# Sliding-window copy: half a batch more through on-chip memory, one opening load, other splits of the direct copies

## The chip, the cores and the metric

The kernel runs on one core of a Trainium2 chip. The metric is device time in microseconds; "before" is quoted as the median of its runs. They were taken in four groups, and the same kernel takes 745 to 755 us from one group to another, so every kernel is compared only with runs of its own group. I call the group of the prediction group 0 (before: 751.7 us) and the three groups of experiments 1, 2 and 3.

## The reference

```
batch, length, dim = 32, 4096, 256        # float32; window_size 64, stride 32
n_windows = (length - window_size) // stride + 1        # 127
for i in range(n_windows):
    result[:, i] = x[:, i * 32 : i * 32 + 64]
```

Each batch is 128 blocks of 32 rows (32 KB each). A window is two neighbouring blocks, so nearly every block is written twice: 134 MB come in, 266 MB go out, nothing is computed.

## The kernel before

Two kinds of copying run side by side. **Direct** batches (21 of 32) go from HBM to HBM, issued on the SP queue, 16 windows at a time, in packets of 32 KB. **Staged** batches (11) are loaded once into on-chip memory (SBUF) and stored twice, on the ACT queue, in packets of 16 KB. The leftovers of the direct batches, 15 windows each ("remainders"), are issued last, on the POOL queue.

```
def load(self, q, g):                          # staged: one tile of 128 blocks
    ...
    parts = [(k, 4, 32, 1) for k in range(4)] if g == 0 else [(0, step, n, step)]
    for rows in parts:                         # (first partition, step, count, unit)
        self.issue(self.c.load(q, self.tiles[i], b, c, rows), self.loaded[i])
...
staged = [*range(1, B, 3)]
...
for i, (b, w) in enumerate(sixteens):          # direct: groups of 16 windows
    loading = turns < first_loads or 0 <= second < loads
    share += 120 if turns < 16 or -8 <= second < 16 else 90 if loading else 18
    if share >= 120:                           # split: two DMAs of 16 packets of 32 KB
        share -= 120
        turns += 4
        count(c.windows(ring_d, b, w, 16, 0), done)
        count(c.windows(ring_d, b, w, 16, 1), sem)
    else:                                      # whole: one DMA of 32 packets of 32 KB
        turns += 3
        count(c.windows(ring_d, b, w, 16), sem)
...
ring_r.wait_ge(near, 16)                       # remainders, when the direct groups are nearly done
for b, w, n in edges:
    ...
    count(c.windows(ring_r, b, w, n), rest)
```

`turns` counts packets, in sixteens. The semaphore write at the end of a DMA is a packet too: on the SP and ACT queues the trace has 3264 and 656 packets of 4 bytes for 204 and 41 DMAs, 16 for each. So a split group is 4 sixteens of packets for its 1024 KB and a whole one 3. The two queues passed packets about one for one: from 120 to 400 us 3294 (SP) and 3292 (ACT), semaphore writes included (2078 and 3100 without them), though one moved 67.61 MB and the other 50.79 (lines below). At that pace packets per byte set each queue's part of the bytes: a split group moves fewer direct bytes per turn than a whole one, and the staged queue gets more of the time. A hand count that alternates packets, with durations from the trace (1.235 and 0.62 us), puts the last packet at 743.5 us, and the trace has it at 745.8 us.

## Time and profile before

| | before, group 0 |
|---|---|
| time, median | 751.7 us |
| DMA bytes | 313.26 MB |
| HBM read and written | 488.0 MB |
| first and last data packet | 2.4 and 745.8 us |

From the page of before, the lines on the DMA engines in 40 slices (DMA is the busy share in tenths), the packets, the queues (q1 is SP, q10 is ACT, q0 is POOL) and HBM:

```profile
DMA  8999999999999999999999999999999999999996
...
DMA packets 18290, 313.26 MB, mean 418 GB/s; under 512 B 4336, under 2 KB 4336, under 8 KB 4528
...
HBM read 220.95 MB, written 267.09 MB: 651 GB/s over the span
```

The engines are busy between the first slice and the last (busy share 1.00 to 1.02 in the stretches below), so time is bytes over rate. The same by stretch (us from the start; then length, POOL busy, clock, DMA busy share, GB/s). A packet is counted whole where it starts, so a short stretch can show a few per cent too much, as a busy share of 1.02 tells. The stretches from 32 and 425 us are those of staged loads, those from 120 and 540 us of staged stores, that from 660 us of the remainders:

```profile
14.00:32.00 18.00, 0.00 (x0) 1.00 1.02 400
32.00:120.00 88.00, 0.00 (x0) 1.00 1.01 428
120.00:400.00 280.00, 0.00 (x0) 1.00 1.01 423
425.00:520.00 95.00, 0.00 (x0) 1.00 1.00 429
540.00:650.00 110.00, 0.00 (x0) 1.00 1.01 422
660.00:735.00 75.00, 6.95 (x13) 1.00 1.01 420
```

The rate is lower where direct copies have a larger part: 428 and 429 GB/s in the load stretches, 423 and 422 in the store stretches. The DMA view of before for 120 to 400 us (queue, packets, MB, share of the engines) shows direct at 67.61 of 118.40 MB, 57%; in the load stretches it is 53%:

```profile
q1 hardware_dynamic: 3294, 67.61, 57.4%
q10 hardware_dynamic: 3292, 50.79, 43.2%
```

**How I add up a trace.** A packet's time has a shortest common value for its size: 1.213 us for 32 KB, 0.611 for 16 KB, 0.159 for 4 KB, 0.084 for 2 KB, 0.009 for a semaphore write. The sum of these over all packets, divided by 16 engines, I call the *floor*; what packets take above it, also over 16, the *excess*. Idle engine time at the start and at the end (fewer than 16 packets under way) comes on top; overlap (more than 16 under way) comes off. For before: floor 729.6 + excess 15.0 + idle 5.3 - overlap 4.1 = 745.8 us, the last packet. The floor depends on bytes and packet sizes alone. Each sum is of one traced run. The five or six runs of one kernel in its group spread over 0.5 us (before_again) to 4.9 us (no_half), so a difference of 1 us in excess between two single traces shows little unless others repeat it. The span ends 3.6 us after that packet; of these the SP queue waits 1.7 us for POOL's and 0.6 us for PE's.

### The profile page before, as it was taken

How to read it: one execution, taken by the hardware profiler on the slowest of the kernel's cores; microseconds unless marked ns; L12 is line 12 of the kernel's file. 1: busy time of each engine (PE TensorE's matmuls, PEld its weight loads, DVE VectorE, ACT ScalarE, POOL GpSimd, SP SyncE). 2: the span in 40 equal slices, each digit the busy share in tenths (PEclk: the TensorE clock that was granted, in tenths of full speed). 3: DMA queues.
4: the chain of work that ended last, by engine and by line, in shares of the span. 5: the costliest groups of instructions: out<-in, count | busy, mean ns of one | idle time of the engine just before them, and what ended most of it. 6: DMA issues, size and time to landing. Idle time of an engine off the chain costs nothing.

```text
span 749.4 us, 322 instructions
## 1 busy us (share of the span) xinstructions
POOL 12.8 (2%) x26
## 2 busy tenths in 40 slices
POOL 0000000000000000000000000000000000040100
DMA  8999999999999999999999999999999999999996
GB/s 360 401 427 429 427 429 428 434 423 418 420 424 423 418 424 415 422 427 427 414 427 417 429 432 429 430 422 430 429 423 421 423 421 419 425 426 423 431 409 262
DMA packets 18290, 313.26 MB, mean 418 GB/s; under 512 B 4336, under 2 KB 4336, under 8 KB 4528
## 3 DMA queue, kind: packets, MB, share of 16 engines
q1 hardware_dynamic: 8016, 154.32, 48.8%
q10 hardware_dynamic: 9104, 138.41, 44.0%
q0 software_dynamic: 1168, 20.51, 6.5%
q14 instruction: 2, 0.02, 0.0%
HBM read 220.95 MB, written 267.09 MB: 651 GB/s over the span
## 4 chain that ended last, share of the span: by engine, by line
another core or an unknown queue 92%; POOL 2%; issue 0%; POOLq 0%; SPq 0%
POOL out_dram L34 2%; POOL out_dram L44 0%; POOLq L236 0%; SPq L172 0%; POOLq L114 0%
## 5 line engine op out<-in xcount | busy, mean ns | idle before, releaser
L34 POOL DMA_DIRECT2D out_dram<-in_x_dram x21 | 12.0, 576 | 691.3 <-DMA out_dram<-in_x_dram 654.0
L44 POOL DMA_DIRECT2D out_dram<-in_x_dram x1 | 0.6, 581 | 0.0
L222 POOL MEMSET const-float32-0.0<- 128x1 f32 x1 | 0.1, 98 | 0.2 <-issue 0.2
L222 POOL MEMSET const-bfloat16-1.0<- 128x1 bf16 x1 | 0.1, 101 | 0.0
L222 POOL MEMSET const-float32-1.0<- 128x1 f32 x1 | 0.1, 98 | 0.0
L222 POOL MEMSET const-uint8-127<- 128x1 uint8 x1 | 0.1, 98 | 0.0
## 6 DMA issues: line engine op xcount, KB each, us to landing
out_dram<-in_x_dram SPq DMA_DIRECT2D x92, 1024.0 KB, 100.7
out_dram<-xb ACTq DMA_DIRECT2D x21, 4096.0 KB, 139.7
out_dram<-in_x_dram SPq DMA_DIRECT2D x110, 512.0 KB, 90.3
xb<-in_x_dram ACTq DMA_DIRECT2D x10, 4096.0 KB, 131.4
out_dram<-in_x_dram POOLq DMA_DIRECT2D x20, 960.0 KB, 38.5
xb<-in_x_dram ACTq DMA_DIRECT2D x4, 1024.0 KB, 15.7
out_dram<-xb ACTq DMA_DIRECT2D x2, 1024.0 KB, 113.4
out_dram<-xb ACTq DMA_DIRECT2D x4, 512.0 KB, 96.9
```

The costliest lines, as they stand in the source:

```text
L34: return q.dma_start(out=self.oap((b * self.nw + w0) * 2 + h, [[2 * blk, n], row]), in_=self.xap(b * self.nb + w0 + h, [[blk, n], row]), m ...
L44: return q.dma_start(out=self.oap((b * self.nw + w0) * 2, [[part, 16], [2 * self.blk, n], row]), in_=self.xap(b * self.nb + w0, [[part, 16 ...
L222: nc = _bacc.Bacc("TRN2", target_bir_lowering=False, num_devices=1)
```

## The change

Its intent: stage half of batch 0 as well, so that fewer bytes pass HBM twice; slow the direct side (more split groups, 73 of 143 instead of 55 of 147, and every third remainder in 16 KB pieces), so that both sides still end together; and load the first tile in one DMA instead of four.

```
-        parts = [(k, 4, 32, 1) for k in range(4)] if g == 0 else [(0, step, n, step)]
-        for rows in parts:
-            self.issue(self.c.load(q, self.tiles[i], b, c, rows), self.loaded[i])
+        self.issue(self.c.load(q, self.tiles[i], b, c, (0, step, n, step)), self.loaded[i])
...
+    items.insert(6, (0, 1, c.nb // 2))
...
-        w = 15 if b - 1 in staged else 0
+        w = c.nb // 2 + 1 if b == 0 else 15 if b - 1 in staged else 0
...            # singles, edges, loads, last columns follow from the half batch
-            share += 120 if turns < 16 or -8 <= second < 16 else 90 if loading else 18
+            share += 120 if turns < 16 or -8 <= second < 16 else 104 if loading else 35
...
-            count(c.windows(ring_r, b, w, n), rest)
+            count(c.windows(ring_r, b, w, n, None, 16384 if i % 3 == 2 else DIRECT), rest)
```

More of the change, by code (lines that the diff above doesn't have):

```diff
@@ L162 @@
     for b in direct:
-        w = 15 if b - 1 in staged else 0
+        w = c.nb // 2 + 1 if b == 0 else 15 if b - 1 in staged else 0
         sixteens += [(b, w + 16 * j) for j in range((c.nw - w) // 16)]
-    singles = [(B - 1, c.nw - 1, 1)]
-    edges = [(b, 0 if b - 1 in staged else 112, 15) for b in direct[:-1]]
+    singles = [(0, 0, 0), (0, c.nb // 2, 1), (B - 1, c.nw - 1, 1)]
+    edges = [(b, 0 if b - 1 in staged else 112, 15) for b in direct[1:-1]] + [(0, 113, 14)]
     last = B - 2
-    edges.append((last, 112, 4))
-    first_loads, loads, stores = 6 * 17, 5 * 17, 6 * 34
+    edges.append((last, 112, 5))
+    first_loads, loads, stores = 6 * 17, 5 * 17 + 9, 6 * 34
     turns = share = 0
@@ L192 @@
         ring_r.wait_ge(near, 16)
-        for b, w, n in edges:
+        for i, (b, w, n) in enumerate(edges):
             for k in (b - 1, b + 1):
@@ L196 @@
                     st.wait_stored(ring_r, place[k])
-            count(c.windows(ring_r, b, w, n), rest)
-        count(c.columns(ring_r, last, 116, 9), rest)
+            count(c.windows(ring_r, b, w, n, None, 16384 if i % 3 == 2 else DIRECT), rest)
+        count(c.columns(ring_r, last, 117, 8), rest)
         st.wait_stored(ring_d, place[B - 1])
```

## The prediction

> **What bounds it now.** Nothing computes; the 16 DMA engines do. The page's DMA row is 9 in 38 of 40 slices; by stretch (busy share and rate per window) DMA is 100% busy from 14 us to 735 us and all packets have ended at 746 us[...]. So time = bytes / rate plus about 2.4 us before the first packet and 3 to 4 us of tail. 313.26 MB move, 418 GB/s mean. HBM itself sees 488 MB (651 GB/s), as a direct byte is read and written there, while a staged byte touches HBM once per transfer.
>
> The rate is not one number. In the two load stretches (32 to 120, 425 to 520 us) it is 428 to 429 GB/s, with the direct queue moving 53% of the bytes; in the store stretches (120 to 400, 540 to 650) 422 to 423 with 57%; during the remainders (660 to 735) 420 with 58%. Single packets say the same: a 32 KB direct one takes 1.216 to 1.218 us in the loads, 1.240 to 1.245 in the stores, 1.249 with the remainders; staged 16 KB ones 0.616 to 0.628; the shortest common values are 1.213 and 0.611. Between 655 and 659 us, staged alone, every packet takes 0.611. So the more direct traffic in the mix, the slower each packet, by 2 to 3%. That waiting is what the change can win. [...]
>
> **What it adds and removes.**
> - Half a batch more is loaded first: 64 x 32 KB = 2.10 MB more DMA bytes (315.36 MB). At 420 GB/s: +5.0 us, all critical, since the engines are never idle. A count of alternating packets with the trace's durations (1.235 and 0.62 us) gives 743.5 us for before's last packet (746 in the trace) and 748.7 for after: +5.1 us.
> - HBM bytes fall by 2.10 MB; the direct share of all bytes falls from 55.8% to 54.1%.
> - More direct groups split in two halves (73 of 143, was 55 of 147): the direct queue moves fewer bytes per turn. Store stretches fall by about 1.6 points of share, loads by 0.8.
> - A third of the remainders in 16 KB pieces: the mean share there falls by about 4 points.
>
> Gain: the two kinds of stretch give 1.4 GB/s per point, perhaps 2 on the steep side. Stores: 2.3 to 3.2 GB/s over 405 us is 2.2 to 3.1 us; remainders 1.3 us (4 to 7 GB/s over 85 us); loads 0.3 us. Together about 4 to 4.7 us.
> - Opening load in one DMA: saves about 2 us of issue on the ACT queue[...]. From 16 to 30 us staged packets take 0.72 to 0.85 us; if that belongs to the first whole-tile load it moves earlier. Worth within 1 us.
>
> Balance: the count has the staged queue end 5 us after the remainders; as it still feeds all engines this costs little.
>
> **Predicted:** 751.0 us, 80% between 747 and 755. Faster by over 2%: 0.01; same: 0.98; slower: 0.01.
>
> **What would show it.** 315.36 MB; store stretches at 425 to 426 GB/s and 32 KB packets near 1.230; remainders at 424 or more; loads unchanged; last packet near 745 us; tail no longer.
>
> **What would make it wrong.** If packets in store stretches stay at 1.24 us, the full 5 us shows (756). If they fall to 1.22, 747. A tail in which one queue alone, or few engines, remain; a worse opening.

## The result, and the profile after

752.87 us against 751.74 us, medians of six runs each. The ratio is 1.0009, interval 0.9987 to 1.0031: the same. (A ratio is the mean time of one kernel's runs over that of the other's of the same rounds, so not quite the ratio of the medians.) The page of after:

```profile
DMA  9999999999999999999999999999999999999996
...
DMA packets 19042, 315.36 MB, mean 420 GB/s; under 512 B 4626, under 2 KB 4626, under 8 KB 4834
...
HBM read 218.86 MB, written 267.09 MB: 647 GB/s over the span
```

Its stretches, and the queues for 120 to 400 us:

```profile
14.00:32.00 18.00, 0.00 (x0) 1.00 1.03 435
32.00:120.00 88.00, 0.00 (x0) 1.00 1.00 426
120.00:400.00 280.00, 0.00 (x0) 1.00 1.01 423
425.00:520.00 95.00, 0.00 (x0) 1.00 1.01 427
540.00:650.00 110.00, 0.00 (x0) 1.00 1.01 425
660.00:735.00 75.00, 3.96 (x7) 1.00 1.00 421
```

```profile
q1 hardware_dynamic: 3426, 65.67, 56.0%
q10 hardware_dynamic: 3423, 52.68, 44.6%
```

More bytes at a slightly better mean rate. The large step is not where I looked for it: it is the opening (400 to 435 GB/s), while the long store stretch did not move. The sums, in us per engine:

| trace | floor | excess (to 35 us / 35 to 650 / later) | idle start + end | last packet |
|---|---|---|---|---|
| before, group 0 | 729.6 | 15.0 (2.2 / 10.5 / 2.3) | 2.6 + 2.6 | 745.8 |
| after, group 0 | 734.8 | 12.2 (0.8 / 9.8 / 1.6) | 2.3 + 2.5 | 747.7 |

So 5.2 us of bytes were added and 2.8 us of waiting taken away: half from the opening, a quarter each from the long middle and from the remainders. In the two store stretches alone, the excess fell from 8.4 to 7.9 us.

### The profile page after: what moved, and what is told of

Its sections match the earlier page's. It is cut to its first block, busy times and chain, and to the rows that moved or that the text cites. A ratio compares the mean times of both kernels' runs of the same rounds, so it can differ in the third digit from the quotient of the medians.

```text
span 751.2 us, 338 instructions
## 1 busy us (share of the span) xinstructions
POOL 12.8 (2%) x26
## 4 chain that ended last, share of the span: by engine, by line
another core or an unknown queue 92%; POOL 2%; issue 0%; POOLq 0%; SPq 0%
POOL out_dram L34 2%; POOL out_dram L44 0%; POOLq L235 0%; SPq L171 0%; POOLq L112 0%
```

## The experiments

My theory: the half batch costs its 5.2 us everywhere, and the other three parts each take away some waiting and keep the ends together. Rivals: a part does nothing, the gain is chance, or the half batch alone does the work.

### Group 1: one part alone or undone (before 754.88 us)

**open_one**: before, with the opening load in one DMA.

```
-        parts = [(k, 4, 32, 1) for k in range(4)] if g == 0 else [(0, step, n, step)]
-        ...
+        self.issue(self.c.load(q, self.tiles[i], b, c, (0, step, n, step)), self.loaded[i])
```

> The kernel before with only the opening load changed to one DMA. Theory (the four strided opening loads make the first whole-tile load slow: packets of 0.72 to 0.85 us between 16 and 30 us, which the changed kernel lacks): 14 to 32 us runs near 430 GB/s instead of 400, the sum of packet time above the shortest durations falls by about 1.4 us per engine in the first 35 us, and the time is 750.2 to 750.6 us against 751.7. Rival (the opening's gain is by chance or is given back later): 751.7 us, within 0.3.

754.74 us, ratio 1.0002 (0.9987 to 1.0017). The opening is fast, as expected (stretch view of this run), and excess to 35 us is 1.0 us:

```profile
14.00:32.00 18.00, 0.00 (x0) 1.00 1.01 429
```

The total did not follow. In this trace the direct queue gets its first packet at 5.7 us, not at 2.4 us as in before. In the two traces of group 0 the order differs the same way: with one load the staged packets start at 2.0 us and the direct ones at 5.7 us, with four loads the direct ones start at 2.4 us and the staged ones at 4.0 us. The remainders start at 664.5 us (658.7 in before of group 0), and excess after 650 us is 3.6 us, the highest of this group, with direct copies in the majority at the end. That the opening's gain was given back there is the likely reading. It was not isolated, as group 1 has no trace of before.

**four_back**: the changed kernel, with the opening in four loads again.

> The changed kernel with the opening load in four strided DMAs again. Theory: 1.4 us slower than the changed kernel, 754.1 us, with 14 to 32 us near 400 GB/s. Rival (the fast opening of the changed kernel comes from the other split of the direct side, not from the load): as the changed kernel, 752.7 us.

754.23 us, ratio to before 0.9996 (0.9982 to 1.0010). The changed kernel itself was not in this group, so the expected difference in time was not tested. The trace was read: 412 GB/s from 14 to 32 us, excess to 35 us 1.7 us, against 0.8 to 1.0 us in the three kernels of this group with one load. The slow opening follows the four loads, not the other parts of the change. This kernel serves below as the reference of group 1 for the middle and the end.

```profile
14.00:32.00 18.00, 0.00 (x0) 1.00 1.02 412
660.00:735.00 75.00, 3.96 (x7) 1.00 1.01 429
```

**pieces_off**: the changed kernel with all remainders in 32 KB pieces.

```
-            count(c.windows(ring_r, b, w, n, None, 16384 if i % 3 == 2 else DIRECT), rest)
+            count(c.windows(ring_r, b, w, n, None, DIRECT), rest)
```

> The changed kernel with all remainders in 32 KB pieces. Theory (smaller pieces lower the direct share, hence packets wait less): 660 to 735 us falls towards the 420 GB/s of before, excess packet time after 650 us rises by about 0.7 us per engine: 753.4 us. Rival (the pieces serve the balance of the ends alone): the remainders end some 7 us before the staged queue by my count (737 and 749 us at unchanged packet times), the staged queue ends alone with packets of 0.611 us, and the time is 752.7 us or less.

757.82 us, ratio 1.0041 (1.0024 to 1.0057). The stretch view has the remainders back at the old rate:

```profile
660.00:735.00 75.00, 4.13 (x8) 1.00 1.00 419
```

Excess after 650 us is 2.9 us, against 1.1 us in four_back: the pieces do take waiting away, more than the 0.7 us expected. And the rival was right about the order of the ends, but wrong about its price: the staged queue ends last and alone (752.0 us, the remainders at 748.2), with at most one packet at a time in its last 3 us, and idle time at the end is 5.5 us against 2.7.

**shares_back**: the changed kernel with the old shares of split groups.

```
-            share += ... 104 if loading else 35
+            share += ... 90 if loading else 18
```

> The changed kernel with the old shares of split groups (90 and 18 of 120). Theory (the lower direct share of the mix speeds up the store stretches): excess packet time in the store stretches rises by 0.5 to 1.5 us per engine, the direct side ends about 10 to 15 us before the staged side, partly made up by staged packets alone at 0.611 us: 753 to 754 us. Rival (the slow packets come in bursts that the mix doesn't govern): 752.7 us, within 0.3.

758.64 us, ratio 1.0060 (1.0038 to 1.0081). Excess from 35 to 650 us is 12.7 us, against 10.2 in four_back and 9.9 in pieces_off, the same bytes on the same chip: splitting more groups takes some 2.5 us of waiting away. Of these, 1.0 to 1.4 us are in the two store stretches, as the theory had it. The rest of the expectation missed: the kernel is 3.8 us slower than before, not 1.3 to 2.3, and the direct side ends 2 to 4 us before the staged side, not 10 to 15. Here too the staged queue ends alone, and the idle time at the end is 4.6 us.

### Group 2: the half batch alone, the opening, a rebalanced mix (before 745.16 us)

**after_again**: the changed kernel, unchanged.

> The changed kernel once more, on the same chip as the others of this group, as the chips of the two earlier groups differ (before took 751.7 us on one and 754.9 us on the other). Theory (the changed kernel's sum is 5.2 us more bytes against about 3 us less waiting, wherever it runs): 0.5 to 2 us slower than before. Rival (waiting differs from chip to chip; where before waits more, the lower direct share wins more): same as before or up to 2 us faster where before takes 754 us or more. The slow spell at 330 to 400 us of its first trace (excess 2.4 us per engine) comes back at the same place if it is of the kernel, and does not if it is chance.

747.87 us, ratio 1.0037 (1.0025 to 1.0049): slower by 0.4%, with an interval clear of 1. The 2.7 us by the medians are more than the 0.5 to 2 us expected; the rival spoke of a before at 754 us or more, which this group does not have. In this group packets wait far less: excess 5.0 us in all, against 12.2 in group 0. The spell at 330 to 400 us has 0.8 us, not the 2.4 us of group 0, so at that size it is not of the kernel.

**half_alone**: of the change, only the half batch (four loads, old shares, no small pieces).

> The changed kernel with the opening in four loads, the old shares and no small pieces, so the half batch alone. Theory (the other parts of the change only put the ends back together and lower the waiting): shortest-duration sum 5.2 us above before, the direct side through about 19 us before the staged side by count at unchanged packet times (730 against 749), excess as before or 1 us less, tail idle 4 to 6 us instead of 2.6: 7 to 10 us slower than before. Rival (the half batch by itself lowers the waiting as it takes the direct traffic off): 3 to 5 us slower.

751.45 us, ratio 1.0080 (1.0063 to 1.0097): 6.3 us slower by the medians, a little less than the theory's range and more than the rival's. The direct groups are through earlier, the remainders start at 638.9 us (650.3 in after_again), the staged queue ends last at 747.2 us (the remainders at 744.6, not 19 us earlier), and idle time at the end is 5.9 us against 4.3. Excess is 8.3 us against 5.0 in after_again: the half batch alone does not bring the low waiting of the whole change. Before has no trace in this group; in group 3, at nearly the same time, its excess is 7.7 us.

**open_rows**: before, each of the four opening loads on 32 consecutive partitions.

```
-        parts = [(k, 4, 32, 1) for k in range(4)] if g == 0 else ...
+        parts = [(32 * k, 1, 32, 1) for k in range(4)] if g == 0 else ...
```

> The kernel before with its opening still in four loads, but each of 32 consecutive partitions instead of every fourth. Theory A (the stride is to blame for slow staged packets at 16 to 30 us): 14 to 32 us near 430 GB/s. Theory B (four small loads ahead of the whole ones, with the direct queue getting its first packets at 2.4 us instead of 5.7, set the engines' phase so that the first whole load is slow): 14 to 32 us at 400 to 412 GB/s again. Time within 1 us of before in both cases.

750.93 us, ratio 1.0076 (1.0057 to 1.0095). Both theories fell, and the time is outside what either allowed:

```profile
2.00:14.00 12.00, 0.00 (x0) 1.00 1.01 276
14.00:29.00 15.00, 0.00 (x0) 1.00 1.03 336
32.00:120.00 88.00, 0.00 (x0) 1.00 1.00 431
```

(This trace is of the slowest of six runs, 2.5 us above the median.) Staged packets take 1.02 us on average until 29 us, and 0.613 us from there to 40 us. The last of the four loads lands at 30.9 us. This made me look again at before: its four loads land at 9.6, 15.2, 20.6 and 27.7 us, the one load of the changed kernel at 20.8 us. So the slow packets of 16 to 27.7 us in before are the third and fourth opening load themselves. They are not "the first whole-tile load", as the prediction and my first expectation had it; only those from 28 to 32 us (0.71 us) are of that load. The timeline shows the same from the other side: the first store waits for that tile, and the ACT queue issues it at 27.75 us in before,

```profile
27.75 22.24 ACTq L63 DMA_DIRECT2D out_dram<-xb  x1
```

and at 20.81 us in after:

```profile
20.81 15.46 ACTq L63 DMA_DIRECT2D out_dram<-xb  x1
```

Most of these 7 us are not slow packets, though. In group 3 the staged packets of before take 0.63 us from 16 to 28 us, hardly more than the shortest, and its first store is still issued at 26.07 us, against 20.86 in after_same. There, too, the direct queue gets its first packet earlier with four loads (2.4 us, with one load 5.6).

In this trace the loads of 32 consecutive partitions are slow from the start: 276 GB/s from 2 to 14 us, where the loads of every fourth partition have 396 in before of group 0 and 395 in group 3. By my count of its packets it moves 208 to 213 GB/s from 2 to 6 us, with no direct packets running yet. Why is not shown. Nor is it shown why the loads of every fourth partition are slow in group 0, from the third on (400 GB/s from 14 to 32 us, 435 with one load), and hardly in group 3 (422 and 437); the trace does not tell which engine a packet ran on.

**open_bal**: open_one with fewer split groups (72 and 12 of 120), so that the late direct side catches up.

> The kernel before with one opening load, and fewer split groups (72 and 12 of 120), so that the direct side, which starts 3.3 us later with the one load, is through earlier. Theory (the opening's gain of 1.2 us was given back because the direct side ended alone, with excess of 2.8 us after 700 us against 1.4): both sides end together again, excess after 700 us near 1.5, and the time is 1 to 2 us below before. Rival (the higher direct share takes the gain back in the store stretches): within 0.5 us of before.

744.78 us, ratio 0.9991 (0.9977 to 1.0004). The two sides end together (739.5 and 739.2 us), excess after 700 us is 0.8 us, but the time is within noise of before. Of the two theories the rival holds: about 0.4 us by the medians is no win that five rounds can show. Its reason holds too, on single traces: excess from 35 to 650 us is 6.3 us, against 5.4 in open_rows, which has before's shares.

### Group 3: both kernels traced on one chip, no half batch, no staging (before 745.30 us)

**before_again** and **after_same**: the two kernels, unchanged.

> The kernel before once more, to have its trace on the same chip as the changed kernel's[...]. Sum of shortest packet times 729.8 us per engine on any chip; excess between 8 us (a quiet chip) and 19 us; time 745 to 755 us. Theory: excess here is the number that sets what the change costs.

> The changed kernel on the same chip as the kernel before. Theory (5.2 us more bytes against waiting that shrinks in proportion, by 20 to 35%, with one opening load, lower direct share and smaller remainders): excess 3 to 5 us less than before where before has 15 to 18 us (time 0 to 2 us above before), 2.5 to 3 us less where before has 8 to 9 us (time 2 to 3 us above before). Rival (the gain is a fixed amount that doesn't depend on the chip): excess 2.8 us less, time 1 to 1.5 us above, whatever before's excess.

745.57 us (ratio 1.0005) and 748.03 us (1.0038, interval 1.0026 to 1.0050). Their sums:

| trace | floor | excess (to 35 us / 35 to 650 / later) | idle start + end | last packet |
|---|---|---|---|---|
| before, group 3 | 729.6 | 7.7 (1.0 / 5.0 / 1.7) | 2.7 + 4.3 | 740.2 |
| after, group 3 | 734.8 | 5.5 (0.8 / 3.4 / 1.3) | 2.2 + 4.0 | 742.2 |

The same +5.2 us of floor, and 2.2 us less excess. The time came out where the theory put it (2 to 3 us above), but the loss of excess is smaller than either expectation: 2.2 of 7.7 us here and 2.8 of 15.0 in group 0 are neither a fixed amount nor a fixed part. The stretches of the store side, before:

```profile
120.00:400.00 280.00, 0.00 (x0) 1.00 1.00 427
540.00:650.00 110.00, 0.42 (x1) 1.00 1.00 427
660.00:735.00 75.00, 2.30 (x4) 1.00 1.00 420
```

and after:

```profile
120.00:400.00 280.00, 0.00 (x0) 1.00 1.01 428
540.00:650.00 110.00, 3.84 (x7) 1.00 1.00 428
660.00:735.00 75.00, 3.70 (x7) 1.00 1.01 424
```

Why packets wait half as long here as in group 0 (another chip or another neighbour, say), nothing I ran shows.

**no_half**: one opening load, the new shares, the small pieces, but eleven staged batches.

> Everything of the change but the half batch: one opening load, shares 104 and 35, small pieces, with eleven staged batches. Theory (the half batch is there to keep the two sides ending together once the direct side is slowed): the staged side ends some 12 to 14 us before the direct side (730 and 744 us by count at unchanged packet times), the direct side alone has long packets (1.3 us or more per 32 KB), excess falls by 2 us or more up to 700 us but comes back after it; time within 1.5 us of before. Rival (the half batch is dead weight): no_half keeps the lower excess and is 2 to 5 us faster than before.

750.88 us, ratio 1.0074 (1.0057 to 1.0091). The rival falls, and of the theory only the order of the ends holds. It is 5.6 us slower than before, not within 1.5. The excess up to 700 us did not fall by 2 us or more: it is 6.5 us, in before_again 6.2 (from 35 to 650 us it is 4.7 against 5.0). Nearly all staged packets are through by about 716 us and the remainders run on alone until 748.7 us, 30 us after the staged side and not 12 to 14. (This trace is of the slowest of six runs, 3.1 us above the median, so its tail is longer than the usual one.)

```profile
660.00:705.00 45.00, 12.70 (x22) 1.00 1.01 422
705.00:716.00 11.00, 0.00 (x0) 1.00 1.05 390
716.00:740.00 24.00, 0.00 (x0) 1.00 0.96 318
```

In that last stretch 32 KB packets take 1.56 us on average and the rate is 318 GB/s; excess after 650 us is 7.6 us against 1.7, and idle time at the end 7.7 us against 4.3. Once the direct side has been slowed, the half batch pays for itself by taking work off it: with it (after_same) the time is 2.9 us shorter.

**direct_only**: before without staging, every window copied from HBM to HBM, no group split.

> No staging at all: every window copied straight, 266 MB of packets instead of 313 MB, 32 batches. If packets kept 1.213 us per 32 KB it would take about 625 us. Theory (packets wait because HBM serves every direct byte twice): with direct traffic alone the HBM rate stays near the 650 to 680 GB/s of the mix, packets take 1.5 to 1.65 us, time 780 to 830 us. Rival (waiting comes from bursts that have nothing to do with the HBM rate): packets near 1.25 us, about 650 us.

809.56 us (one run, one look), as the theory expected; the rival's 650 us falls. The engines move only 266 MB, floor 618.7 us, but excess is 177 us:

```profile
100.00:700.00 600.00, 0.00 (x0) 1.00 1.00 334
```

```profile
HBM read 266.34 MB, written 266.34 MB: 659 GB/s over the span
```

334 GB/s read and as much written is 668 GB/s at HBM, steady for 600 us; the median 32 KB packet takes 1.55 us. In before_again, of the same group, the long store stretch has 57.0% direct traffic in 427 GB/s, so HBM serves 1.570 x 427 = 671 GB/s there, nearly the same:

```profile
q1 hardware_dynamic: 3327, 68.20, 57.3%
q10 hardware_dynamic: 3327, 51.36, 43.1%
```

In before of group 0 it is 1.571 x 423 = 665 GB/s; the load stretches there need 1.53 x 428 = 655 GB/s, and packets are close to the floor (32 KB in 1.216 to 1.218 us). So I read some 665 to 671 GB/s as what HBM serves this core. That is an inference from the two rates being alike: no run tells it from a limit of HBM-to-HBM copies as such.

**What the traces say together.** The direct share of the bytes from 35 to 650 us, counted from the packets, and the excess there:

| group | trace | direct share, % | excess, us |
|---|---|---|---|
| group 1 | open_one | 55.8 | 13.7 |
| group 1 | shares_back | 55.2 | 12.7 |
| group 1 | four_back | 54.7 | 10.2 |
| group 1 | pieces_off | 54.6 | 9.9 |
| groups 2, 3 | open_bal | 56.1 | 6.3 |
| groups 2, 3 | open_rows | 55.8 | 5.4 |
| groups 2, 3 | before_again | 55.7 | 5.0 |
| groups 2, 3 | half_alone | 55.3 | 5.2 |
| groups 2, 3 | no_half | 54.9 | 4.7 |
| groups 2, 3 | after_same | 54.3 | 3.4 |
| groups 2, 3 | after_again | 54.2 | 3.1 |

With one small exception, the lower the direct share, the less the packets wait: about 1.4 us per point of share in groups 2 and 3 and about 3 in group 1 (straight lines through these points), but only 0.6 in the pair of group 0, which had the slow spell. The half batch alone (5.2 us) and the other parts alone (4.7) hardly differ from before (5.0) in single traces; both together (3.4 and 3.1) do.

## Why the prediction was right or wrong

The time was right: 751.0 us predicted, 747 to 755 as the range, 752.87 measured; "same" was given 0.98.

- **What bounds it**: right. The engines are busy throughout in both traces (busy share 1.00 to 1.03 in the stretches from 14 to 735 us). direct_only points, by inference, to a second limit behind the packets' waiting, HBM at about 668 GB/s, which the prediction did not name.
- **"+5.0 us, all critical"**: right. The floor rose by 5.2 us in groups 0 and 3.
- **"Stores ... 2.2 to 3.1 us"**: right mechanism (less direct traffic, less waiting: the table above), but far too large. In the two store stretches the excess fell by 0.5 us in group 0 and by 0.8 us in group 3. From 35 to 650 us, loads included, it fell by 0.7 and by 1.6 us; undoing the shares alone gave 2.5 us back in group 1. The stated signs failed: 120 to 400 us stayed at 423 GB/s instead of 425 to 426, and 32 KB packets of the two store stretches took 1.246 and 1.236 us (1.240 and 1.245 before), not 1.230. The prediction had said of just this case that "the full 5 us shows (756)"; it did not, not least because the opening and the remainders gave 2.1 us. The loads, which were to gain 0.3 us, lost 0.4 in group 0 and stayed in group 3. In group 0 a slow spell at 330 to 400 us cost 1.0 us more than before had there; it did not come back at that size.
- **"Remainders 1.3 us"**: 0.7 us in group 0, 0.4 in group 3, about 1.8 by undoing it in group 1. Right in kind, too large for the pair predicted. The stretch reached 421 GB/s, not 424.
- **"Opening ... worth within 1 us"**: too small for group 0 (1.4 us); 0.7 to 0.9 us in group 1 and 0.2 in group 3. The reason given was wrong: the slow packets belonged for the most part to the four opening loads, not to the first whole-tile load, and so they were not moved earlier but removed.
- **"Together about 4 to 4.7 us"**: that sum was of stores, remainders and loads. Of these, 1.4 us came in group 0 and 2.0 in group 3. The opening, outside the sum, gave 1.4 us more in group 0, so 2.8 us in all. That covers the miss of the centre: 5.2 - 2.8 = 2.4 us, less 0.6 us of idle and overlap, is the 1.8 us by which the last packet came later. I predicted "near 745 us" for it; it came at 747.7 us. That the time lay well inside the range is in part luck: the largest gain was too big by a factor of four or more, and an opening worth more than predicted made up for part of it.
- **"The staged queue end 5 us after the remainders ... costs little"**: the count was wrong, as both ended within 2 us in group 0 (745.8 and 747.7 us). The step "costs little" also failed where that ending did occur: 2 to 3 us more idle time in pieces_off and shares_back.

Why a change that does what it intends does not win: an estimate from the runs, argued and not isolated by any of them. It takes direct_only's rate for a limit on every chip. At the 668 GB/s of direct_only, before's 488.0 MB at HBM take 731 us and after's 485.9 MB take 727 us. The engines' floor less overlap is 725.5 us before and 730.5 us after. By this estimate the kernel before already stands where the two limits cross. The change takes 3 to 4 us off one and puts 5 us on the other.

## What to carry to other kernels

When two resources are both near their limit, price a trade on both sides: here 5.2 us of engine time against, by the estimate, 3 to 4 us of HBM time. Two queues that share engines should end together: where one ran on alone at the end (pieces_off, shares_back, half_alone, no_half), the idle time there was 1.6 to 3.3 us longer. So test a part of a rebalancing change only with the balance restored, or read its trace rather than its time. When groups of runs differ by more than the effect, put both kernels in every group.
